# Scale and shift of the first normalisation: the conditioning product moved from GpSimd and VectorE to TensorE for five of eight tiles

## The chip, the cores and the metric

The kernel runs on one core of a Trainium2 chip. The metric is the device time of one execution in microseconds (us); three runs of the kernel before are given below, and one execution was profiled.

## The reference, cut to what matters

One decoder layer on x of shape (1, 1024, 1024) in float32. A conditioning vector c of 1024 numbers makes six vectors of 1024; the first two of them shift and scale the first normalisation, and what comes out goes into a wide projection:

```python
c_act = jax.nn.silu(c)
mod = c_act @ w_ada[l] + b_ada[l]                 # (1, 6*1024)
sh1, sc1, gt1, sh2, sc2, gt2 = jnp.split(mod, N_MOD, axis=-1)
h = _rmsnorm(x, norm1_g[l]) * (1.0 + sc1) + sh1
proj = h @ w_in[l]                                # RWKV, attention and gate columns
...                                               # two mixers, an output projection, an MLP
```

Only `sh1` and `sc1` are touched by the change: 2 x 1024 columns of `w_ada`, 8 MB, each summed over 1024 rows with `c_act` as weights.

## The kernel before, in words

The channels (1024) are cut into eight tiles of 128, numbered k = 0 to 7, and the same 1024 rows of `w_ada` into eight pieces j. For each k the kernel does, in this order:

- `ada_load(k)` loads the tile `wa`k: for each of the eight pieces j, 128 rows by 2 x 128 columns (scale, shift), in two transfers of 512 KB on SP's queue. `wa` has three buffers, so the fourth load waits for the first tile to be used up.
- `ada_sum(k)` makes the two sums. GpSimd multiplies three of the eight pieces by `cact` in one instruction (L277) and adds them into one (L279, two instructions); VectorE multiplies and adds the other five (L283, L285) into `acc`. TensorE then sums `acc` over its 128 partitions by two matmuls against a column of ones, one for scale and one for shift, each with one output column (`gp<-ones,acc`; L41 is the helper `mm` through which all matmuls but transposes go). VectorE turns `gp` into the two columns of `gs`k (L292, L293).
- `modulate(k)` transposes the normalised x of tile k on TensorE (eight 128x128 transposes into `xp`, L302), ScalarE evicts them with scale and shift from `gs`k into `hr` (L303), casts that to `hhi` (L304), and VectorE makes the remainder `hlo` (L305).
- `products(k)` adds tile k's share to three projections that are kept open in PSUM over all eight tiles: `p_wa`, `p_r` and `p_k`, each as hi x hi, lo x hi and hi x lo in two halves, 18 matmuls of 512 columns.

The loop calls `ada_sum(k+1)` and `modulate(k+1)` ahead of `products(k)`; a scheduler then sets the final order on each engine. Four PSUM banks of the tag `ps` serve `gp`, both halves of `xp` and `p_r`; two of them are held by `p_r` throughout, so `gp` and the halves of `xp` take turns in the other two. When the eight tiles are through, TensorE goes on with the projection `p_v`.

In the profile a float32 matmul appears as two MATMUL rows and two LDWEIGHTS rows (two matmuls `gp<-ones,acc` of a tile are four rows); a transpose, and a matmul on the split operands, is one.

Of the kernel before, what the change touches and what calls it, by code (L numbers as in the profile page):

```python
# [8 lines left out]
F32 = mybir.dt.float32  # L9
# [4 lines left out]
ALU = mybir.AluOpType  # L14
AX = mybir.AxisListType

P = 128
S = 1024
D = 1024
KT = 8  # L20
# [15 lines left out]
def build(ctx, tc, A, out):  # L36
    nc = tc.nc
    PE, ACT, DVE, POOL, SP = nc.tensor, nc.scalar, nc.vector, nc.gpsimd, nc.sync

    def mm(o, l, r, start, stop):  # L40
        PE.matmul(o, l, r, start=start, stop=stop)  # L41

    def pool(**kw):
        if kw.get("space") != bass.MemoryType.DRAM:
            kw["reuse_waits"] = "tile"
        return tc.tile_pool(**kw)
# [16 lines left out]
    def big(name, tag="pp"):  # L63
        return pools[tag][0].tile([P, pools[tag][1]], F32, tag=tag, name=name)

    def bank(name, tag="ps"):
        return big(name, tag)

    def halves_of(o):
        return [o[:, 0:512], o[:, 512:1024]]  # L70
# [7 lines left out]
    ones = const.tile([P, P], F32, name="ones")  # L78
# [47 lines left out]
    def vcol(name, i=0, n=1):  # L126
        vc, o = col[name]
        return vc[:, o + i : o + i + n]
# [9 lines left out]
    def small(name, n=1):  # L138
        return const.tile([P, n], F32, name=name)
# [5 lines left out]
    cact = small("cact", 8)  # L145
# [6 lines left out]
    def rsqrt(o, v, scale, eps, tmp, n):  # L152

        a, b = tmp[:, 0:n], tmp[:, n : 2 * n]
        ACT.activation(o, v, AF.Sqrt, bias=eps, scale=scale)
        DVE.tensor_scalar(a, v, scale, eps, ALU.mult, ALU.add)
        DVE.reciprocal(o, o)
        DVE.tensor_tensor(b, o, o, ALU.mult)
        DVE.tensor_tensor(b, b, a, ALU.mult)
        DVE.tensor_scalar(b, b, -0.5, 1.5, ALU.mult, ALU.add)  # L160
        DVE.tensor_tensor(o, o, b, ALU.mult)
# [21 lines left out]
    def win(c0, n=P):  # L183
        return w_in[:, :, c0 : c0 + n]
# [41 lines left out]
    with pool(name="st", bufs=1) as st:  # L226
        ssq = st.tile([P, 8], F32, name="ssq")
        rs1 = st.tile([P, 8], F32, name="rs1")
        rtmp = st.tile([P, 16], F32, name="rtmp")
        xs, was, gs, firsts = [], [], [], []  # L230

        def x_load(t):
            xt = st.tile([P, D], F32, name=f"x{t}")
            SP.dma_start(xt, x_t[t])
            xs.append(xt)

        def ada_load(k):
            wa = st.tile([P, KT, 2, P], F32, tag="wa", name=f"wa{k}", bufs=3)
            SP.dma_start(wa[:, :, 0, :], w_ada[:, :, D + k * P : D + (k + 1) * P])
            SP.dma_start(wa[:, :, 1, :], w_ada[:, :, k * P : (k + 1) * P])  # L240
            was.append(wa)

        def first_load(name, parts, to):
            raw = to.tile([P, KT, P], F32, tag="wraw", name=f"wr_{name}", bufs=2)
            for i, part in enumerate(parts):
                w_ = P // len(parts)
                SP.dma_start(raw[:, :, i * w_ : i * w_ + w_], part)
            return raw

        def first_tile(name, raw, to, banks):  # L250
            hi = to.tile([P, KT, P], F32R, tag="whi", name=f"wh_{name}", bufs=2)
            lo = to.tile([P, KT, P], F32R, tag="wlo", name=f"wl_{name}", bufs=2)
            ACT.copy(hi, raw)
            DVE.tensor_tensor(lo, raw, hi.bitcast(F32), ALU.subtract)
            o = [bank(f"p_{name}{hf}") for hf in range(2)] if banks else halves_of(big(f"p_{name}"))
            firsts.append(((hi, lo), o))

        def normalise(g):
            ts = slice(4 * g, 4 * g + 4)
            for t in range(4 * g, 4 * g + 4):  # L260
                junk = st.tile([P, D], F32, tag="junk", name=f"jk{t}", bufs=2)
                ACT.activation(junk, xs[t], AF.Square, accum_out=ssq[:, t : t + 1])
            rsqrt(rs1[:, ts], ssq[:, ts], 1.0 / D, eps1, rtmp, 4)
            for t in range(4 * g, 4 * g + 4):
                r = rs1[:, t : t + 1]
                if g:
                    ACT.activation(xs[t], xs[t], AF.Copy, scale=r)
                else:
                    DVE.tensor_scalar(xs[t], xs[t], r, None, ALU.mult)

        NPOOL = 3

        def ada_sum(k):

            wa, c0 = was[k], KT - NPOOL
            rest = wa[:, c0:].rearrange("p k i n -> p k (i n)")
            POOL.tensor_tensor(rest, rest, cact[:, c0:].unsqueeze(2).broadcast_to([P, NPOOL, 2 * P]), ALU.mult)  # L277
            for j in range(c0 + 1, KT):
                POOL.tensor_tensor(wa[:, c0], wa[:, c0], wa[:, j], ALU.add)  # L279
            acc = st.tile([P, 2, P], F32, tag="acc", name=f"acc{k}", bufs=3)  # L280
            for j in range(c0):
                if j == 0 and k == 0:
                    DVE.tensor_scalar(acc, wa[:, j], cact[:, j : j + 1], None, ALU.mult)  # L283
                else:
                    DVE.scalar_tensor_tensor(acc, wa[:, j], cact[:, j : j + 1], acc if j else wa[:, c0], ALU.mult, ALU.add)  # L285
            gp = bank(f"gp{k}")
            for i in range(2):
                mm(gp[:, i : i + 1], acc[:, i, :], ones[:, 0:1], True, k > 0)
                if k == 0:
                    mm(gp[:, i : i + 1], wa[:, c0, i, :], ones[:, 0:1], False, True)  # L290
            g_ = st.tile([P, 2], F32, name=f"gs{k}")
            DVE.tensor_scalar(g_[:, 0:1], gp[:, 0:1], bsc1[:, k : k + 1], vcol("g1", k), ALU.add, ALU.mult)  # L292
            DVE.tensor_scalar(g_[:, 1:2], gp[:, 1:2], vcol("bsh1", k), None, ALU.add)  # L293
            gs.append(g_)

        def modulate(k):
            hr = st.tile([P, S], F32, tag="hr", name=f"hr{k}", bufs=2)
            for hf in range(2):
                sl = slice(hf * 512, hf * 512 + 512)
                xp = bank(f"xp{k}_{hf}")  # L300
                for t in range(4):
                    PE.transpose(xp[:, t * P : (t + 1) * P], xs[4 * hf + t][:, k * P : (k + 1) * P], ident)  # L302
                ACT.activation(hr[:, sl], xp, AF.Identity, bias=gs[k][:, 1:2], scale=gs[k][:, 0:1])  # L303
            ACT.copy(hhi[:, k, :], hr)  # L304
            DVE.tensor_tensor(hlo[:, k, :], hr, hhi[:, k, :].bitcast(F32), ALU.subtract)  # L305

        def products(k):
            for w, o in firsts:
                for a, b in ((0, hhi), (1, hhi), (0, hlo)):
                    for hf in range(2):  # L310
                        sl = slice(hf * 512, hf * 512 + 512)
                        mm(o[hf], w[a][:, k, :], b[:, k, sl], k == 0 and a == 0 and b is hhi, k == KT - 1 and b is hlo)

        for t in range(8):
            x_load(t)
        ada_load(0)
        raws = [first_load("wa", [win(COL_WD, 64), win(COL_AD, 64)], st)]
        raws.append(first_load("r0", [win(COL_R)], st))
        raws.append(first_load("k0", [win(COL_K)], wp))
        ada_load(1)  # L320
        normalise(0)
        normalise(1)
        ada_sum(0)
        first_tile("wa", raws[0], st, False)
        modulate(0)
        first_tile("r0", raws[1], st, True)
        first_tile("k0", raws[2], wp, False)
        for k in range(KT):
            if k + 1 < KT:
                if k:  # L330
                    ada_load(k + 1)
                ada_sum(k + 1)
                modulate(k + 1)
            products(k)
            if k == 5:
                omu, hbase, kmh, kmo = second_columns()
# [759 lines left out]
    raw1, first, sums, rest = {}, {}, {}, {}  # L1096
# [368 lines left out]
    with pool(name="fr", bufs=1, side="right") as fr, pool(name="fp", bufs=1) as fp:  # L1465
        raws = {"B21": nx["b"]}
        acc = []
# [130 lines left out]
        for s, (g, i) in enumerate(flat):  # L1598
# [7 lines left out]
            tag, opens, _, _, to = STEPS[i]  # L1606
# [49 lines left out]
```

## Time and profile before

| | us |
|---|---|
| three runs: median (lowest to highest) | 1697.89 (1694.49 to 1701.91) |
| the profiled execution's own time | 1695.92 |
| its span in the trace | 1694.2 |
| TensorE busy, of the span | 1597.7 (94%) |
| VectorE, ScalarE, GpSimd busy | 1129.7, 731.2, 356.2 |

The span is what the trace covers from the first to the last instruction; 1.7 us of the time lie outside it. The busy time of TensorE counts matmuls whose ends are modelled, so durations of single matmuls overlap: the cost of one in a row of its kind is read from start to start. [...]

### The profile page before, as it was taken

To read this page: it belongs to the slowest core of one execution; us is meant where nothing else is said; L and a number is where in the kernel's file an instruction comes from. 1 tells how busy PE (TensorE), PEld (TensorE's weight loads), DVE (VectorE), ACT (ScalarE), POOL (GpSimd) and SP (SyncE) were. 2 spreads that over 40 slices of the span, in tenths; PEclk is the share of its full clock that TensorE was granted. 3 is DMA by queue.
4 is the path that set the end of the run, shared out by engine and by line. 5 is a ranking of instruction groups with operands and counts; after the bars stand their busy time and mean duration, and the time that the engine had idled before them with its cause. 6 is when DMAs were issued, how large, how long until landed. Compare 5 with 4: busy or idle time off the path is not lost.

```text
span 1694.2 us, 21870 instructions
## 1 busy us (share of the span) xinstructions
PE 1597.7 (94%) x8293; PEld 1277.9 (75%) x8293; DVE 1129.7 (67%) x1685; ACT 731.2 (43%) x1138; POOL 356.2 (21%) x353
## 2 busy tenths in 40 slices
PE   3999998999999999999999999999999969999997
PEld 2767766777777878888887787777777857888886
DVE  6677665556665735666647655975555569899978
ACT  5454432444454723333233334755555524433334
POOL 4410000699992011121110000122211100000000
PEclk9999999999999999999999999999999989999999
DMA  8535333622223168778767421344444474364522
GB/s 248 139 100 152 114 121 124 154 55 68 62 79 108 42 193 250 225 234 240 231 210 242 168 100 63 126 157 150 147 156 160 149 274 160 124 224 154 170 75 100
DMA packets 217111, 256.24 MB, mean 151 GB/s; under 512 B 30097, under 2 KB 156330, under 8 KB 216878
## 3 DMA queue, kind: packets, MB, share of 16 engines
q1 hardware_dynamic: 205390, 214.71, 41.6%
q0 software_dynamic: 11408, 39.85, 6.2%
q8 instruction: 65, 1.06, 0.3%
q14 instruction: 40, 0.33, 0.1%
q10 hardware_dynamic: 208, 0.28, 0.0%
HBM read 178.16 MB, written 72.45 MB: 148 GB/s over the span
## 4 chain that ended last, share of the span: by engine, by line
PE 62%; issue 14%; DVE 7%; DMA 6%; POOL 3%; ACT 2%; SPq 0%; POOLq 0%; DVEq 0%; ACTq 0%
PE x L1215 11%; PE y L1215 8%; PE p_gb L41 5%; PE p_out L41 5%; PE p_ga L41 3%; POOL f_d L1230 3%; PE my L41 3%; PE p_fk L41 3%; PE p_ob L41 3%; PE p_fq L41 2%; PE p_fv L41 2%; PE yv L41 2%; PE p_v L41 2%; PE p_r L41 2%; PE tp L819 2%
## 5 line engine op out<-in xcount | busy, mean ns | idle before, releaser
L1404 ACT CAST dh<-dA 128x1024 fp32r<-128x1024 f32 x54 | 56.3, 1046 | 148.0 <-PE x L1215 72.2
L1215 PE MATMUL x<-wh,dh 128*128 128x512 f32 x256 | 102.1, 399 | 14.5 <-ACT wh L1093 14.5
L639 POOL TENSOR_TENSOR dg<-dg,inv 128x62 f32<-128x62 f32 (+30 forms) x62 | 100.2, 1617 | 4.8
L1215 PE MATMUL x<-wl,dh 128*128 128x512 f32 x256 | 100.9, 395 | 0.0
L1215 PE MATMUL x<-wh,fl 128*128 128x512 f32 x256 | 100.1, 391 | 0.0
L638 POOL TENSOR_TENSOR inv<-dg 128x62 f32<-128x62 f32 (+30 forms) x62 | 92.9, 1498 | 4.9
L1583 DVE TENSOR_TENSOR fl<-dA,dh 128x1024 fp32r<-128x1024 f32 x54 | 65.2, 1218 | 20.7 <-ACT dh L1404 14.7
L1215 PE MATMUL y<-wh,dh 128*128 128x512 f32 x176 | 69.4, 394 | 0.0
L1215 PE MATMUL y<-wl,dh 128*128 128x512 f32 x176 | 68.6, 393 | 0.6 <-DVE wl L1094 0.6
L1215 PE MATMUL y<-wh,fl 128*128 128x512 f32 x176 | 68.3, 388 | 0.0
L1215 PEld LDWEIGHTS x<-wh,dh 128*128 128x128 f32 x256 | 48.8, 191 | 24.6 <-ACT wh L1093 14.9
L823 DVE TENSOR_TENSOR pl<-tp,ph 128x512 fp32r<-128x512 f32 (+1 forms) x80 | 49.1, 631 | 24.8 <-ACT ph L822 24.6
L879 DVE CUSTOM_DVE_ANT_0 pt<-s,cb 128x512 f32<-128x512 f32 (+2 forms) x64 | 36.4, 584 | 37.4 <-PE s L41 36.5
L881 ACT ACTIVATE pt<-pt,sm 128x128 f32<-128x128 f32 (+3 forms) x64 | 49.5, 775 | 24.5 <-DVE sm L879 23.5
L701 POOL TENSOR_TENSOR sw<-sbd,wcs 64x256 f32<-64x256 f32 x28 | 22.8, 816 | 169.1 <-DVE sbd L702 138.4
L1239 ACT ACTIVATE ff<-ff 128x512 f32<-128x512 f32 x48 | 30.3, 632 | 64.7 <-DVE ff L1325 29.3
L1215 PEld LDWEIGHTS x<-wl,dh 128*128 128x128 f32 x256 | 48.3, 189 | 12.0 <-DVE wl L1094 0.5
L1215 PEld LDWEIGHTS x<-wh,fl 128*128 128x128 f32 x256 | 48.7, 190 | 10.7
L822 ACT CAST ph<-tp 128x512 fp32r<-128x512 f32 (+1 forms) x80 | 41.5, 543 | 29.2 <-PE tp L819 27.6
L41 PE MATMUL p_out<-h_wo,hhi 128*128 128x512 f32 x128 | 50.8, 397 | 2.2 <-ACT h_wo L1050 2.2
L41 PE MATMUL p_gb<-hhi,wl_gb 128*128 128x512 f32 x128 | 51.4, 402 | 0.2 <-DVE wl_gb L178 0.2
L819 PE MATMUL tp<-ident,pt 128*128 128x128 f32 x288 | 49.6, 282 | 2.2 <-ACT pt L881 1.8
(584 smaller groups left out, 4909.5 us busy)
## 6 DMA issues: line engine op xcount, KB each, us to landing
dA<-f_d SPq DMA_DIRECT2D x27, 1024.0 KB
aw<-in_w_ada SPq DMA_DIRECT2D x32, 512.0 KB
ur<-in_w_ff SPq DMA_DIRECT2D x30, 512.0 KB
B<-in_w_ff SPq DMA_DIRECT2D x15, 1024.0 KB
f_d<-ff POOLq DMA_DIRECT2D x48, 256.0 KB, 4.1
wa<-in_w_ada SPq DMA_DIRECT2D x16, 512.0 KB
sc_d<-scb SPq DMA_DIRECT2D x16, 512.0 KB
sct<-sc_d SPq DMA_DIRECT2D x16, 512.0 KB
```

What stands on the lines that cost most here:

```text
L41: PE.matmul(o, l, r, start=start, stop=stop)
L638: POOL.tensor_tensor(tv, dg[:, 0:s, s : s + 1].broadcast_to([P, s, m]), dg[:, s : s + 1, s + 1 :].broadcast_to([P, s, m]), ALU.mult)
L639: POOL.tensor_tensor(dg[:, 0:s, s + 1 :], dg[:, 0:s, s + 1 :], tv, ALU.add)
L819: PE.transpose(tp[:, x * P : (x + 1) * P], pr[b][:, t * P : (t + 1) * P], ident)
L822: ACT.copy(ph[:, 0:w_], tp[:, 0:w_])
L823: DVE.tensor_tensor(pl[:, 0:w_], tp[:, 0:w_], ph[:, 0:w_].bitcast(F32), ALU.subtract)
L879: DVE.tensor_tensor_reduce(pt[:, c0:c1], sv, cb[:, c0:c1], -0.125, low, ALU.add, ALU.min, st_[:, x : x + 1])
L881: ACT.activation(pt[:, 0:n], pt[:, 0:n], AF.Exp, bias=low, scale=-1.0, accum_out=ls[:, b : b + 1])
L1215: PE.matmul(o, l, r, start=start, stop=stop, skip_group_check=True)
L1230: POOL.dma_start(f_d[AOPS.index(name), j], src)
L1404: ACT.copy(hs[i], src[:, 2 * i : 2 * i + 2])
L1583: DVE.tensor_tensor(fl[:, sl], src[:, sl], f32(hs[i_]), ALU.subtract)
```

## The change

TensorE multiplies `w_ada`'s pieces by the conditioning itself for tiles 0, 1, 3, 5 and 7: 16 matmuls with one output column each (eight pieces, scale and shift), the piece as the loaded operand and a column of `cact` as the moving one. For tiles 2, 4 and 6 VectorE does all eight pieces (eight instructions where there were five) and TensorE the two matmuls against ones as before. GpSimd does none. `wa` gets a fourth buffer and `acc` loses one; tiles 1 to 3 are loaded ahead of the loop, and the load of tile k+4 comes after the sum of tile k+1.

```diff
         def ada_load(k):
-            wa = st.tile([P, KT, 2, P], F32, tag="wa", name=f"wa{k}", bufs=3)
+            wa = st.tile([P, KT, 2, P], F32, tag="wa", name=f"wa{k}", bufs=4)
...
-        NPOOL = 3
-
         def ada_sum(k):
-            wa, c0 = was[k], KT - NPOOL
-            rest = wa[:, c0:].rearrange("p k i n -> p k (i n)")
-            POOL.tensor_tensor(rest, rest, cact[:, c0:].unsqueeze(2).broadcast_to([P, NPOOL, 2 * P]), ALU.mult)
-            for j in range(c0 + 1, KT):
-                POOL.tensor_tensor(wa[:, c0], wa[:, c0], wa[:, j], ALU.add)
-            acc = st.tile([P, 2, P], F32, tag="acc", name=f"acc{k}", bufs=3)
-            for j in range(c0):
-                if j == 0 and k == 0:
-                    DVE.tensor_scalar(acc, wa[:, j], cact[:, j : j + 1], None, ALU.mult)
-                else:
-                    DVE.scalar_tensor_tensor(acc, wa[:, j], cact[:, j : j + 1], acc if j else wa[:, c0], ALU.mult, ALU.add)
+            wa = was[k]
             gp = bank(f"gp{k}")
-            for i in range(2):
-                mm(gp[:, i : i + 1], acc[:, i, :], ones[:, 0:1], True, k > 0)
-                if k == 0:
-                    mm(gp[:, i : i + 1], wa[:, c0, i, :], ones[:, 0:1], False, True)
+            if k < 2 or k % 2:
+                for i in range(2):
+                    for j in range(KT):
+                        mm(gp[:, i : i + 1], wa[:, j, i, :], cact[:, j : j + 1], j == 0, j == KT - 1)
+            else:
+                acc = st.tile([P, 2, P], F32, tag="acc", name=f"acc{k}", bufs=2)
+                for j in range(KT):
+                    if j == 0:
+                        DVE.tensor_scalar(acc, wa[:, j], cact[:, j : j + 1], None, ALU.mult)
+                    else:
+                        DVE.scalar_tensor_tensor(acc, wa[:, j], cact[:, j : j + 1], acc, ALU.mult, ALU.add)
+                for i in range(2):
+                    mm(gp[:, i : i + 1], acc[:, i, :], ones[:, 0:1], True, True)
...
-        ada_load(1)
+        for k in (1, 2, 3):
+            ada_load(k)
...
         for k in range(KT):
             if k + 1 < KT:
-                if k:
-                    ada_load(k + 1)
                 ada_sum(k + 1)
+                if k + 4 < KT:
+                    ada_load(k + 4)
                 modulate(k + 1)
```

The order moves on TensorE. The first place is the start of the stage, from the sums of tile 0 to those of tile 1. Before, TensorE ran twelve matmuls of tile 0's products while VectorE and GpSimd made tile 1's sums:

```order
L302 MATMUL xp0_1_228<-ident_72,x7_146 128x128
L41 MATMUL p_wa_220<-hhi_124,wh_wa_216 128x512 x2
L41 MATMUL p_wa_220<-hhi_124,wl_wa_217 128x512 x2
L41 MATMUL p_k0_246<-hhi_124,wh_k0_242 128x512 x2
L41 MATMUL p_wa_220<-hlo_125,wh_wa_216 128x512 x2
L41 MATMUL p_k0_246<-hhi_124,wl_k0_243 128x512 x2
L41 MATMUL p_k0_246<-hlo_125,wh_k0_242 128x512 x2
L41 MATMUL gp1_256<-ones_77,acc1_250 128x1 x2
L302 MATMUL xp1_0_263<-ident_72,x0_132 128x128
```

In the changed kernel there stands at the same place:

```order
L299 MATMUL xp0_1_237<-ident_72,x7_146 128x128
L41 MATMUL p_wa_229<-hhi_124,wh_wa_225 128x512
L41 MATMUL gp1_256<-cact_118,wa1_158 128x1 x8
L299 MATMUL xp1_0_280<-ident_72,x0_132 128x128
L299 MATMUL xp1_0_280<-ident_72,x1_134 128x128
L299 MATMUL xp1_0_280<-ident_72,x2_136 128x128
L299 MATMUL xp1_0_280<-ident_72,x3_138 128x128
L299 MATMUL xp1_1_286<-ident_72,x4_140 128x128
L41 MATMUL gp1_256<-cact_118,wa1_158 128x1 x8
```

Of tile 0's 18 products one now stands ahead of tile 1's sums and transposes and 17 behind them, in one piece; the other twelve no longer fill the time in which tile 1's sums were made.

The second place is tile 3, the first of the later tiles whose sums go to TensorE. Before:

```order
L41 MATMUL p_k0_246<-hlo_125,wh_k0_242 128x512 x2
L41 MATMUL gp3_358<-ones_77,acc3_352 128x1 x2
L302 MATMUL xp3_0_365<-ident_72,x0_132 128x128
L302 MATMUL xp3_0_365<-ident_72,x1_134 128x128
L302 MATMUL xp3_0_365<-ident_72,x2_136 128x128
L302 MATMUL xp3_0_365<-ident_72,x3_138 128x128
L41 MATMUL p_wa_220<-hhi_124,wh_wa_216 128x512 x2
L302 MATMUL xp3_1_371<-ident_72,x4_140 128x128
```

In the changed kernel:

```order
L41 MATMUL p_k0_255<-hlo_125,wh_k0_251 128x512 x2
L41 MATMUL gp3_363<-cact_118,wa3_164 128x1 x16
L299 MATMUL xp3_0_387<-ident_72,x0_132 128x128
L299 MATMUL xp3_0_387<-ident_72,x1_134 128x128
L299 MATMUL xp3_0_387<-ident_72,x2_136 128x128
L299 MATMUL xp3_0_387<-ident_72,x3_138 128x128
L299 MATMUL xp3_1_393<-ident_72,x4_140 128x128
L299 MATMUL xp3_1_393<-ident_72,x5_142 128x128
...
L41 MATMUL p_wa_229<-hhi_124,wh_wa_225 128x512 x2
```

Sixteen one-column matmuls stand where two stood, and all eight transposes of the tile follow them in one piece. Behind tile 7 the order of TensorE's instructions is that of before.

## Rows read from the trace of the kernel before

**Rows 1.** Windows: busy us of PE, PEld, DVE, ACT, POOL; clock, DMA share, GB/s.

```profile
10.00:20.00 10.00, 0.00 (x0) 0.00 (x0) 6.85 (x19) 8.84 (x16) 1.90 (x2) 1.00 1.16 309
...
35.00:40.00 5.00, 1.26 (x6) 0.77 (x5) 4.06 (x4) 0.00 (x0) 4.52 (x5) 1.00 0.00 0
...
55.00:60.00 5.00, 5.00 (x30) 4.24 (x29) 4.60 (x9) 2.28 (x4) 2.10 (x2) 1.00 0.04 11
```

**Rows 2.** Timeline: start, us, engine, instruction, count, [idle before, releaser]; tiles 0 and 1.

```profile
17.95 0.35 DVE L283 TENSOR_SCALAR acc<-wa,cact 128x256 f32<-128x256 f32 x1 [0.60 <-DMA wa<-in_w_ada]
...
23.95 1.95 PE L302 MATMUL xp<-ident,x 128*128 128x128 f32 x8
...
27.48 1.47 POOL L277 TENSOR_TENSOR wa<-wa,cact 128x768 f32<-128x768 f32 x1 [6.11 <-DMA wa<-in_w_ada]
...
28.64 1.22 PE L41 MATMUL p_wa<-hhi,wh_wa 128*128 128x512 f32 x2 [2.75 <-ACT hhi L304]
...
39.23 1.01 PE L41 MATMUL gp<-ones,acc 128*128 128x1 f32 x4 [3.74 <-DVE acc L285]
...
40.11 1.95 PE L302 MATMUL xp<-ident,x 128*128 128x128 f32 x8
...
41.11 2.05 DVE L285 SCALAR_TENSOR_TENSOR acc<-wa,cact,acc 128x256 f32<-128x256 f32 x4
```

**Rows 3.** Timeline of TensorE alone, from tile 0's last products on.

```profile
41.70 1.20 PE L41 MATMUL p_r<-hhi,wh_r 128*128 128x512 f32 x2
...
43.56 1.05 PE L41 MATMUL p_r<-hlo,wh_r 128*128 128x512 f32 x2
44.41 0.62 PE L41 MATMUL p_wa<-hhi,wh_wa 128*128 128x512 f32 x1
44.84 0.53 PE L41 MATMUL gp<-ones,acc 128*128 128x1 f32 x4
45.23 0.64 PE L302 MATMUL xp<-ident,x 128*128 128x128 f32 x4
...
53.25 0.66 PE L302 MATMUL xp<-ident,x 128*128 128x128 f32 x4 [1.70 <-DVE gs L293]
```

**Rows 4.** The same: one whole tile, a wait, the stage's end.

```profile
57.48 0.50 PE L41 MATMUL gp<-ones,acc 128*128 128x1 f32 x4
57.84 0.63 PE L302 MATMUL xp<-ident,x 128*128 128x128 f32 x4
...
62.47 0.63 PE L41 MATMUL p_k<-hlo,wh_k 128*128 128x512 f32 x2
62.94 0.50 PE L41 MATMUL gp<-ones,acc 128*128 128x1 f32 x4
...
65.16 0.66 PE L302 MATMUL xp<-ident,x 128*128 128x128 f32 x4 [0.99 <-DVE gs L293]
...
85.50 0.47 PE L41 MATMUL p_v<-hhi,wh_v 128*128 128x512 f32 x1 [0.16 <-DVE wa_t L446]
```

**Rows 5.** Timeline of TensorE: eight one-column matmuls in a row, much later.

```profile
808.67 1.84 PE L41 MATMUL ac<-ones,aa 128*128 128x1 f32 x16
810.37 1.14 PE L41 MATMUL my<-sbd,art 128*128 128x128 f32 x8
```

**Rows 6.** Windows of 1 us after an idle TensorE; columns as in the first windows.

```profile
165.00:166.00 1.00, 0.00 (x0) 0.00 (x0) 1.00 (x1) 0.00 (x0) 0.00 (x0) 1.00 0.45 163
...
167.00:168.00 1.00, 1.00 (x10) 1.00 (x10) 1.00 (x2) 0.49 (x2) 0.00 (x0) 0.88 0.06 17
168.00:169.00 1.00, 1.00 (x7) 1.00 (x6) 0.03 (x1) 0.58 (x2) 0.00 (x0) 0.50 0.00 0
...
171.00:172.00 1.00, 1.00 (x3) 0.42 (x3) 0.00 (x0) 0.62 (x2) 0.00 (x0) 0.91 0.99 320
```

**Rows 7.** Timeline of TensorE: another idle stretch, then sixteen transposes alone.

```profile
270.23 3.58 PE L593 MATMUL bp<-ident,bk 128*128 128x128 f32 x16 [3.97 <-DVE bk L589]
273.55 0.49 PE L41 MATMUL p_f<-hlo,wfs 128*16 128x512 f32 x1
```

**Rows 8.** Windows of 1 us over those transposes; columns as in the first windows.

```profile
271.00:272.00 1.00, 1.00 (x7) 1.00 (x6) 0.43 (x1) 0.59 (x1) 0.00 (x0) 0.50 0.00 0
...
274.00:275.00 1.00, 1.00 (x6) 0.38 (x4) 0.00 (x0) 0.00 (x0) 0.00 (x0) 1.00 0.99 338
```

## The prediction

> **What bounds the kernel now.** I read the page first: TensorE is busy for 94% of the span, so elsewhere its own work sets the time, and what it is given more to do comes back in the end unless it fills a gap. The change lies in the first 86 us, so I went there by windows. In [rows 1] the reader sees three different pictures: from 10 to 20 us TensorE does nothing while 309 GB/s come in; from 35 to 40 us it works 1.26 us of 5 and the DMA share is 0.00, so it isn't the loads that are waited for there; from 55 to 60 us it is busy without a gap. The timeline tells what ends the waits. Tile 0's coefficients come from `wa0`, whose last half VectorE gets at 17.95; the tile's transposes start at 23.95, its first product at 28.64, released by ScalarE's cast. Tile 1's sums start at 39.23, after 3.74 us of waiting for `acc` [rows 2]. From 41.70 on TensorE runs on, but for two waits for VectorE's `gs`, 1.70 us at 53.25 and 0.99 us at 65.16, until `p_v` begins at 85.50 [rows 3, 4]. So two things count: when tile 1 gets going, and TensorE's work per tile after that.
>
> The clock is part of it. [...]
>
> **The start (tiles 0 and 1).** Tile 0: the sums by VectorE and GpSimd, 17.95 to 22 us, make way for 32 rows on TensorE (16 float32 matmuls, two rows each). At the low level a one-column row costs 0.22 us (four from 39.23 to 40.11 [rows 2]), so 7.0 us, plus eight transposes at 0.20 (40.11 to 41.70 [rows 2, 3]), 1.6: 8.6 us. If both halves of `wa0` are there only at 17.95, this ends at 26.6, against 23.95 + 1.6 = 25.6 now; but the sums of scale need only the first half, 512 KB earlier, 1.7 us at the 309 GB/s of [rows 1], and then it ends at 24.9. I take nothing, bounds -0.7 and +1.0 us.
>
> Tile 1: TensorE starts again at 28.64 and now has one product (0.43), 32 one-column rows (7.0) and eight transposes (1.6) before the other 17 products of tile 0: 37.7. Its tile `wa1` is there by 27.48 [rows 2], and the queue ahead of it is the same. The 17 products: with the low level for 3.1 us more, as from 41.70 to 44.84, 7.4 of them at 0.425, then 9.6 at 0.235, together 5.4: done at 43.1. Now tile 0's last product ends at 44.41. **Term 1: -1.3 us.** Bounds: all 17 at the low level, 7.2, so 44.9 (+0.5); or the clock rising while the one-column rows run, which is a rival below (-4.5).
>
> **The later tiles.** The work per tile is read from 57.48 to 62.94 [rows 4]: 5.46 us, of it 0.36 the four `gp` rows. Tiles 3, 5 and 7 get 32 rows instead. What does one cost at the full level, in a row of many? The nearest row is of exactly this kind, eight one-column matmuls with new loaded operands: 16 rows from 808.67 to 810.37, 0.106 us each [rows 5]. So 32 x 0.106 = 3.4, less 0.36, is 3.04 per tile. **Term 2: +9.1 us.** Bounds: 0.09 a row as in the short groups (0.36 / 4) gives +7.6; 0.22, were the clock low throughout, +20. Tiles 2, 4 and 6 keep their two matmuls.
>
> [...]
>
> **VectorE, GpSimd and the loads.** VectorE's eight multiply-adds of an even tile cost about 0.51 each undisturbed (four in 2.05 us at 41.11 [rows 2]), 4.1 us, and lie under at least one tile's TensorE work of 5.46; without that cover an even tile would wait up to 4.1 us for them. VectorE had five for each of eight tiles and now has 24 in all, and GpSimd none, so `gs` should no longer be late: the waits of 1.70 and 0.99 go. New ones come: the second half of `xp` uses the bank that `gp` leaves, and in tile 3 only four transposes stand between, so TensorE waits for two small VectorE instructions; tile 2's `hlo` also comes closer to its use. I put 1.0 us for all, bounds 0 and 2.7. **Term 3: -1.7 us.** The loads get earlier, into a time when the DMA share was 0.00; `vr_b` and `p_v`'s weights now queue on SP behind the last `w_ada` tile, which waits for tile 3's sums to leave its buffer, and are used only at the stage's end: nothing. GpSimd's work leaves no path.
>
> **Sum.** -1.3 + 9.1 - 1.7 = +6.1 us at the end of the stage. `p_v` follows it with 0.16 us of waiting, and the order behind is unchanged, so it stays: 1695.9 + 6.1 = 1702.0 against the profiled execution's own time. That time is 2.0 below the median of the three runs, from which the sum is 1704.0. I say 1703.
>
> **Rivals.** *The clock falls.* Tiles 3, 5 and 7 now have 3.4 us of one-column rows and then up to eight transposes. After an idle stretch the granted clock fell to 0.50 for 3.4 us (0.88 in the slice from 167, 0.91 in that from 171: 0.24 + 3 + 0.18 [rows 6]); if one-column rows count as little as idling, it falls in each of the three tiles. 3.4 us at half speed cost 1.7: +5.1 in all, 1695.9 + 6.1 + 5.1 = 1707; were all the one-column rows at 0.22, 11 more on the sum, 1713. For it: nothing in the trace has so long a stretch of one column. Against it: 1.7 us of them at 808.67 cost 0.106 a row throughout, and during sixteen transposes alone (270.23 to 273.55) the clock came back from 0.50 to 1.00 [rows 7, 8], so short matmuls that each load an operand do count for something. It decides (slower by over 0.5%, past 1704.4 on the same basis) from the second tile in which it happens. [...] Chance 0.25.
>
> *The clock rises early.* TensorE has no pause from 28.64 on. Before, the full level came 5.6 us after 39.23. If one-column rows count fully, it comes at 34.2: three of the second sixteen rows are through, 13 at 0.106 and the last transposes end at 35.9, 17 products at 0.235 at 39.9, 4.5 ahead of now: -4.5 + 9.1 - 1.7 = +2.9, 1699. Against it: from 39.23 to 41.70 the one-column rows and transposes did not raise it. Chance 0.2.
>
> *The loss is taken up behind the stage.* Then 1696. VectorE idles there at times, but TensorE's waits behind the stage are for chains that start from it; chance 0.08.
>
> Could it be faster by over 0.5%? With the early rise, 0.09 a row and no new wait: -4.5 + 7.6 - 2.7 = +0.4. The best bounds together give no gain, as the three tiles put back what the start saves.
>
> **How the numbers follow.** The sum as it stands has 0.42; 0.05 is left for what I do not see. 0.5% (8.5 us) is about what a measurement here can tell from no change, given that the three runs differ by 7.4. The range goes from the early rise with some spread, 1696, to a fall in most tiles, 1711. Slower by over 0.5%: 0.2 of the falling clock and 0.05 of the sum's upper end, 0.25; faster 0.03; the same 0.72.
>
> **What would show it.** Term 1: tile 0's last product near 43 us, one-column rows of tile 1 at 0.22. Term 2: sixteen matmuls (32 rows) of tiles 3, 5 and 7 in 3.4 us each, clock 1.00. Term 3: no wait for `gs` over 0.5 us. `p_v` should start near 91.6. Wrong would be: a clock of 0.50 between 45 and 90 us, one-column rows far from 0.106, or tile 1's products at 0.235 from the first.

## The result, and the profile after

The changed kernel takes 1711.37 us in the median of eight runs (1706.74 to 1715.47) against 1698.86 for the kernel before, measured beside it (eight runs, 1694.49 to 1705.18): ratio 1.0062, 95% interval 1.0043 to 1.008, so 12.5 us slower by the medians. That is 8 us past the number forecast and at the very end of its range (1696 to 1711, passed by 0.4), on the side of the rival called the falling clock. The forecast gave 0.72 to a change within 0.5% and 0.25 to a kernel slower by more than that; the second is what came.

The profiled execution after took 1715.47, the longest of its eight, and the one before 1695.92, 2.9 under its kernel's median. The two traces are therefore 19.6 us apart where the medians are 12.5 apart. 13.84 of this is there at `p_v`. Behind it the shift is still 14.0 where the transposes `hp` begin (987.3, now 1001.3). Another 5.2 come between `hp` and the first matmul of `x`, a stretch of 398.0 us before and 403.2 after, which took 397.0 to 404.3 over all the profiles here with no order by kernel; it isn't explained here.

The timeline of TensorE after, from tile 0's first product to `p_v`:

```profile
start us, us, engine line op out<-in xcount [idle before <-releaser]
28.09 0.80 PE L41 MATMUL p_wa<-hhi,wh_wa 128*128 128x512 f32 x1 [2.96 <-ACT hhi L301]
28.69 3.41 PE L41 MATMUL gp<-cact,wa 128*128 128x1 f32 x16
31.95 1.31 PE L299 MATMUL xp<-ident,x 128*128 128x128 f32 x5
33.05 3.41 PE L41 MATMUL gp<-cact,wa 128*128 128x1 f32 x16
...
42.33 0.62 PE L41 MATMUL p_k<-hlo,wh_k 128*128 128x512 f32 x2
42.79 0.63 PE L41 MATMUL p_wa<-hhi,wh_wa 128*128 128x512 f32 x2
...
47.80 0.62 PE L41 MATMUL p_k<-hlo,wh_k 128*128 128x512 f32 x2
48.26 4.06 PE L41 MATMUL gp<-cact,wa 128*128 128x1 f32 x32
52.18 1.95 PE L299 MATMUL xp<-ident,x 128*128 128x128 f32 x8
53.78 1.20 PE L41 MATMUL p_wa<-hhi,wh_wa 128*128 128x512 f32 x2
...
65.46 4.18 PE L41 MATMUL gp<-cact,wa 128*128 128x1 f32 x32
...
82.94 4.75 PE L41 MATMUL gp<-cact,wa 128*128 128x1 f32 x32
...
99.34 0.47 PE L41 MATMUL p_v<-hhi,wh_v 128*128 128x512 f32 x1
```

The start is as forecast: the one-column rows of tile 1 cost 0.20 us each (sixteen from 28.69 to 31.95), and tile 0's last product is through at 42.79, where before it was through at 44.41 [rows 3]. After 28.09 no row up to `p_v` has a wait in brackets, the rows left out here included, so the waits for `gs` of 1.70 and 0.99 us [rows 3, 4] are gone. Yet `p_v` starts at 99.34 instead of 85.50. The windows over the same execution show why (the number before the DMA share is the granted clock):

```profile
core 0: us, PE busy (x) PEld busy (x) DVE busy (x) ACT busy (x) POOL busy (x), PEclk, DMA share, GB/s
50.00:51.00 1.00, 1.00 (x11) 1.00 (x11) 0.00 (x0) 0.00 (x0) 0.00 (x0) 1.00 0.00 0
51.00:52.00 1.00, 1.00 (x8) 1.00 (x9) 0.00 (x0) 0.00 (x0) 0.00 (x0) 0.64 0.00 0
52.00:53.00 1.00, 1.00 (x6) 1.00 (x7) 0.64 (x3) 0.00 (x0) 0.00 (x0) 0.50 0.00 0
...
57.00:58.00 1.00, 1.00 (x4) 0.81 (x3) 1.00 (x3) 0.00 (x0) 0.00 (x0) 0.50 0.24 55
58.00:59.00 1.00, 1.00 (x5) 0.82 (x5) 0.04 (x1) 0.00 (x0) 0.00 (x0) 0.95 0.01 2
...
68.00:69.00 1.00, 1.00 (x8) 1.00 (x7) 0.00 (x0) 0.00 (x0) 0.00 (x0) 0.67 0.00 0
...
75.00:76.00 1.00, 1.00 (x5) 0.77 (x4) 0.03 (x1) 0.00 (x0) 0.00 (x0) 0.91 0.00 0
...
85.00:86.00 1.00, 1.00 (x8) 1.00 (x9) 0.00 (x0) 0.00 (x0) 0.00 (x0) 0.71 0.10 20
...
92.00:93.00 1.00, 1.00 (x5) 0.86 (x4) 0.61 (x1) 0.36 (x1) 0.62 (x1) 0.88 0.57 154
```

TensorE is busy for 1.00 of every slice, and still the clock falls to 0.50 three times, once in each of tiles 3, 5 and 7, while the one-column rows run. The slice from 51 has 0.72 us at the low level, those from 52 to 58 six, the slice from 58 0.10: 6.8 us. The other two lows are as long, 20.5 us in all. A pair of products takes 0.86 us at 0.50 (55.63 to 56.49, where every slice reads 0.50) and 0.46 at 1.00 (42.33 to 42.79 above), so about half of a low is lost, by estimate 10.2 us. With the working of the prediction this closes to about a microsecond: -1.6 at the start, +9.1 for the rows, +10.2 for the clock, -2.9 for the waits that are gone (1.70, 0.99 and the 0.16 before `p_v`) make +14.8, measured +13.84.

### The profile page after: what moved, and what is told of

The parts are those of the page before. It is cut to its first block, busy times and chain, and to the rows that moved or that the text cites. A ratio compares the mean times of both kernels' runs of the same rounds, so it can differ in the third digit from the quotient of the medians.

```text
span 1713.8 us, 22086 instructions
## 1 busy us (share of the span) xinstructions
PE 1627.9 (95%) x8429; PEld 1307.5 (76%) x8429; DVE 1111.7 (65%) x1669; ACT 731.5 (43%) x1138; POOL 327.6 (19%) x329
## 4 chain that ended last, share of the span: by engine, by line
PE 65%; issue 14%; DVE 8%; DMA 6%; POOL 3%; ACT 3%; SPq 0%; POOLq 0%; ACTq 0%; DVEq 0%
PE x L1213 11%; PE y L1213 7%; PE p_gb L41 5%; PE p_out L41 5%; PE p_ga L41 3%; POOL f_d L1228 3%; PE my L41 3%; PE p_r L41 3%; PE p_ob L41 3%; PE p_fq L41 2%; PE p_k L41 2%; PE p_fv L41 2%; PE p_fk L41 2%; PE yv L41 2%; PE p_v L41 2%
## 5 line engine op out<-in xcount | busy, mean ns | idle before, releaser
L1213 PE MATMUL y<-wh,fl 128*128 128x512 f32 x176 | 68.3, 388 | 0.0
L41 PE MATMUL p_ga<-hhi,wh_ga 128*128 128x512 f32 x128 | 51.4, 401 | 0.0
```

The lines of the kernel that those rows point to most:

```text
L1213: PE.matmul(o, l, r, start=start, stop=stop, skip_group_check=True)
```

## The experiments

The theory: one-column rows that stand alone for about 3.5 us let the clock fall, and their own price is as forecast. The rivals: the transposes behind them do it, or the float32 operand loads, or the loss is not the clock's but one of VectorE's or of the start. Ratios are to the kernel before, measured beside each. A start of `p_v` is from one execution.

**128 equal columns in place of one, all five tiles.** The moving operand is the same column of `cact` repeated; the matmuls and operand loads are as many, the sums the same.

```diff
+        cb = st.tile([P, KT, P], F32, name="cb")
+        DVE.tensor_copy(cb, cact.unsqueeze(2).broadcast_to([P, KT, P]))
...
-                        mm(gp[:, i : i + 1], wa[:, j, i, :], cact[:, j : j + 1], j == 0, j == KT - 1)
+                        mm(gp[:, i * P : i * P + P], wa[:, j, i, :], cb[:, j, :], j == 0, j == KT - 1)
```

> As the changed kernel, but each of TensorE's sixteen matmuls per tile (tiles 0, 1, 3, 5, 7) moves 128 equal columns (cact repeated) instead of one; same number of rows, same loaded operands. Theory (TensorE's one-column rows do not keep the clock at its full level: 20.5 us at the low level between 51 and 92 us cost some 10 of the 13.8 us that the stage lost): granted clock 1.00 from 45 to 90 us, a row still about 0.11 us, p_v starts at 88 to 91 us instead of 99.3, and the time is 8 to 12 us below the changed kernel's 1711, about 1700. Rival (it is the work of the rows and the longer wait for the coefficients, the clock is a side show): p_v at 99 or later, time 1711 or more.

Measured: 1697.21 us (five runs), ratio 0.9951 [0.9928, 0.9975], `p_v` at 83.42. TensorE's timeline, and windows over tiles 3, 5 and 7:

```profile
41.46 3.74 PE L41 MATMUL gp<-cb,wa 128*128 128x128 f32 x32
45.03 0.60 PE L303 MATMUL xp<-ident,x 128*128 128x128 f32 x4
...
55.73 3.73 PE L41 MATMUL gp<-cb,wa 128*128 128x128 f32 x32
```

```profile
41.00:46.00 5.00, 5.00 (x42) 4.71 (x41) 3.59 (x8) 0.27 (x1) 0.00 (x0) 1.00 0.76 186
55.00:60.00 5.00, 5.00 (x42) 4.79 (x41) 1.72 (x4) 1.05 (x2) 0.00 (x0) 1.00 0.43 115
69.00:75.00 6.00, 6.00 (x48) 5.29 (x47) 1.19 (x8) 0.52 (x1) 0.62 (x1) 1.00 0.00 0
```

32 rows take 3.57 us (41.46 to 45.03), nearly what they take with one column at the full level (3.49, in a profile further down), and the clock stays at 1.00. The operand loads and the transposes are the same, so neither of them let it fall by itself here. The gain went further than expected since the start gained too: tile 0's last product is through at 35.8 instead of 42.8.

**One-column rows in the first two tiles only, and in the later three only.** In the first run tiles 2 to 7, in the second tiles 0 and 1, are again split between VectorE (five pieces) and GpSimd (three); tiles 2, 4 and 6 of the second stay whole on VectorE, as in the changed kernel. The condition of each run (the rest of the edits is left out):

```diff
-            if k < 2 or k % 2:
+            if k < 2:                 # first two
+            if k > 1 and k % 2:       # later three
```

> TensorE makes the sums of tiles 0 and 1 alone; tiles 2 to 7 are shared by VectorE and GpSimd as before. Theory: only the gain of the start is left (tile 0's products end about 1.6 us sooner, no waits for gs), clock 1.00 after 42 us, p_v at 81 to 84 us against 85.5 before, time 1694 to 1699, not to be told from before or a little faster. Rival (the loss comes with the new loading order and the sums of tiles 0 and 1): p_v later than 90 us, time over 1705.

> TensorE makes the sums of tiles 3, 5 and 7 alone; tiles 0 and 1 are shared by VectorE and GpSimd as before; 2, 4 and 6 on VectorE as in the changed kernel. Theory: the whole loss and none of the gain: three stretches at clock 0.50, p_v at 99 to 104 us, time 1710 to 1717. Rival (the sums of tiles 0 and 1 carry the loss): p_v below 90, time about 1700.

Measured: first two 1695.41 us (five runs), 0.9943 [0.9923, 0.9963], `p_v` at 84.55, just past what was expected; the granted clock reads 1.00 up to `p_v` and the waits for VectorE are back (the longest 1.48 for `gs`). Later three 1702.03 us (ten runs), 1.0011 [0.9981, 1.0042], `p_v` at 96.4, three lows, of 3.4, 6.8 and 6.8 us. Both its numbers are below what was expected, the time by 8 us. In part this is because tile 1's sums came to TensorE at 36.1 rather than 39.23 [rows 2] and one low was half as long; the rest isn't explained. At `p_v` the loss is in the later tiles; the time of the second can't be told from the kernel before.

**The operands exchanged**: the column of `cact` is loaded and 256 columns of `w_ada` move, all five tiles; two small matmuls bring the row back to columns.

```diff
+                for j in range(KT):
+                    mm(gp[0:1, 0 : 2 * P], cact[:, j : j + 1], wa[:, j].rearrange("p i n -> p (i n)"), j == 0, j == KT - 1)
+                DVE.tensor_copy(rw, gp[0:1, 0 : 2 * P])
```

> As the changed kernel, but operands swapped: a column of cact is loaded and a piece's 256 columns of w_ada move (16 rows per tile instead of 32), and two small matmuls turn the resulting row back into two columns. Theory (what keeps the clock up is columns that move): a row about 0.12 us, sums of a tile 1.9 us at the full level, clock 1.00 from 40 us on, p_v at 77 to 81 us, time 1690 to 1696. Rival (a matmul that fills one column of the array counts as little as one that moves one column): the clock stays low at the start until the 512-column products come, p_v at 83 to 88 us, time about 1698.

Measured: 1699.74 us (ten runs), 0.9991 [0.9968, 1.0013], `p_v` at 88.49, no low in tiles 3, 5 and 7. `p_v` and the time missed the theory's numbers because the price of a row did. Tile 3's row of the timeline,

```profile
44.57 3.61 PE L41 MATMUL gp<-wa,cact 128*1 128x256 f32 x16
48.12 0.66 PE L303 MATMUL xp<-ident,x 128*128 128x128 f32 x4
```

has 16 rows from 44.57 to 48.12, 0.222 us for 256 columns, where 0.12 was expected. A row of 512 columns on the split operands takes 0.23 (two in 0.46 from 42.33 to 42.79 above). The float32 row of 256 columns thus cost about twice as much per column, and the two rows of a matmul four times.

**The one-column matmuls of tiles 5 and 7 put between the 512-column products**, tile 3's left in one piece.

```diff
                         mm(o[hf], w[a][:, k, :], b[:, k, sl], k == 0 and a == 0 and b is hhi, k == KT - 1 and b is hlo)
+                        if extra is not None:
+                            next(extra, None)
```

> As the changed kernel, but the sixteen one-column matmuls of tiles 5 and 7 are each put between 512-column products of an earlier tile; those of tile 3 still stand in one piece. Same work. Theory: the clock falls once, in tile 3 (some 6.8 us at 0.50), and not in tiles 5 and 7; p_v at 91 to 94 us, time about 1704. Rival (work alone): p_v at 98 to 100, time 1711.

Measured: `p_v` at 93.28, as expected; one low, from 50.5 to 57.3, in tile 3's rows and behind them, none in tiles 5 and 7. This is one profile, with two such stretches. Windows over these two:

```profile
62.00:69.00 7.00, 7.00 (x50) 6.45 (x49) 3.76 (x8) 2.17 (x3) 0.00 (x0) 1.00 0.50 138
76.00:90.00 14.00, 14.00 (x82) 11.92 (x82) 4.62 (x11) 5.00 (x6) 2.90 (x6) 1.00 0.32 79
```

The time, 1710.7 us (seven runs; 1.0042 [1.0007, 1.0077]), was a miss by 7: `p_v` came 6 us earlier than in the profile after (0.8 earlier than in the second one, below), and the median gained nothing that can be told. The stretch from `hp` to `x` was 403.0 us in its profile; what else came back isn't known.

**The start alone, two more ways**: 128 columns, and exchanged operands, for tiles 0 and 1; the rest split as before.

> TensorE makes the sums of tiles 0 and 1 alone, with 128 moving columns per row; tiles 2 to 7 are shared by VectorE and GpSimd as before. Theory: the early clock of the run with 128 columns (tile 0's products done at 35.8 us) without the 3 x 3.2 us of rows in tiles 3, 5 and 7, so p_v at 74 to 78 us and a time of 1688 to 1693, below both kernels. Rival (VectorE and GpSimd then set the pace, their sums take as long as a tile): waits for gs of 1 to 3 us per tile, p_v at 80 to 84, time 1695 to 1699.

> TensorE makes the sums of tiles 0 and 1 alone, with swapped operands (a column of cact loaded, 256 columns moving); tiles 2 to 7 are shared by VectorE and GpSimd as before. Theory: half as many rows at the start, so tile 1's sums end sooner than with 128 equal columns; p_v at 73 to 77 us, time 1687 to 1692. Rival (VectorE and GpSimd set the pace, or the clock does not rise early): p_v at 80 to 84, time 1695 to 1699.

Measured: 1694.21 (0.9964 [0.9944, 0.9985], `p_v` 82.1) and 1694.82 (0.9965 [0.9938, 0.9992], `p_v` 84.4), twelve runs each. Both missed on `p_v`, and the rival came: TensorE, now early, waited for VectorE. Behind such waits the clock fell as well, in the first from 37.9 to 44.7 (TensorE had waited 2.09 us to 37.69), though not after the longest wait there, 2.91 us to 56.60; in the second at 42.0 and at 52.2 for 3.4 us each. TensorE's waits in the first (us in total, times, longest):

```profile
PE xp L305 <- DVE gs L296: 2.9, 1, 2.9
PE p_wa L41 <- DVE hlo L308: 2.1, 1, 2.1
...
PE gp L41 <- DVE acc L290: 2.0, 1, 2.0
```

**Half of the columns each**: 128 columns in tiles 0 and 1 alone, then in tiles 3, 5 and 7 alone; the sums are divided among engines as in the changed kernel.

```diff
-                        mm(gp[:, i : i + 1], wa[:, j, i, :], cact[:, j : j + 1], j == 0, j == KT - 1)
+                        n = P if k < 2 else 1              # start;  P if k > 1 and k % 2 else 1  for later
+                        mm(gp[:, i * n : i * n + n], wa[:, j, i, :], cb[:, j, 0:n], j == 0, j == KT - 1)
```

> The changed kernel with 128 equal moving columns in the scale and shift matmuls of tiles 0 and 1 alone; tiles 3, 5 and 7 keep one column. It splits the gain of the kernel with 128 columns throughout (p_v at 83.4 us against 99.3) between the start and the later tiles. Theory (the one-column rows let the clock fall wherever they stand alone for 3 us or more, and at the start they also keep it from rising): at the start the full level comes near 29 us and tile 0's last product near 35 instead of 42.3; three stretches at 0.50 of about 7 us each remain in tiles 3, 5 and 7, 3.4 us of loss each, so p_v at 91 to 94 and a time of 1702 to 1707. Rival (what the earlier start gains is given back, because VectorE's sums of tiles 2, 4 and 6 are then late): p_v at 97 or later, with waits of TensorE for acc or gs of 2 us or more. If an earlier full clock keeps the gate from falling later, p_v comes near 84.

> The other half: one column in tiles 0 and 1 as in the changed kernel, 128 equal columns in tiles 3, 5 and 7. Theory: the start is as in the changed kernel, with tile 0's last product near 42.3 us; no stretch at 0.50 after it; the sixteen matmuls of tiles 3, 5 and 7 take 3.6 us each as with 128 columns throughout; p_v at 88 to 91 and a time of 1698 to 1703. Rival (the fall comes from the eight transposes that follow the rows, or from the wait for gs, not from the one-column rows): the stretches at 0.50 stay and p_v is later than 95. This kernel and the one with 128 columns in tiles 0 and 1 alone should together give the 15.9 us that 128 columns throughout gained at p_v.

Measured: start 1701.77 us (ten runs), 1.0019 [0.9997, 1.0042]; later 1701.52 (ten runs), 1.0018 [0.9998, 1.0038]. Of the changed kernel's 1.0062 the first takes back 0.43% and the second 0.44%, and both together (the kernel with 128 columns throughout) 1.1%. The second came as expected. TensorE's timeline in it:

```profile
47.72 3.73 PE L41 MATMUL gp<-cb,wa 128*128 128x128 f32 x32
...
62.10 3.73 PE L41 MATMUL gp<-cb,wa 128*128 128x128 f32 x32
...
76.59 3.84 PE L41 MATMUL gp<-cb,wa 128*128 128x128 f32 x32
...
89.89 0.47 PE L41 MATMUL p_v<-hhi,wh_v 128*128 128x512 f32 x1
```

No stretch is at 0.50 up to `p_v`, and `p_v` is 4.4 us behind the kernel before. The first was a miss: `p_v` at 85.53, not 91 to 94, because only tile 7's rows were followed by a low. That is nearer to the last possibility named for it, that an earlier full clock keeps the clock from falling later. Tiles 3 and 5, with the same rows as in the changed kernel, ran at 1.00. Tile 3's rows in the timeline, then windows:

```profile
42.36 3.63 PE L41 MATMUL gp<-cb,wa 128*128 128x1 f32 x32
45.85 0.63 PE L304 MATMUL xp<-ident,x 128*128 128x128 f32 x4
```

```profile
42.00:46.00 4.00, 4.00 (x37) 3.91 (x36) 1.12 (x1) 0.00 (x0) 0.00 (x0) 1.00 0.66 161
56.00:60.00 4.00, 4.00 (x36) 3.90 (x35) 0.02 (x1) 0.00 (x0) 0.00 (x0) 1.00 0.77 213
74.00:75.00 1.00, 1.00 (x10) 0.93 (x10) 0.47 (x5) 0.00 (x0) 0.00 (x0) 1.00 0.00 0
75.00:76.00 1.00, 1.00 (x6) 0.84 (x5) 0.22 (x3) 0.57 (x1) 0.71 (x1) 0.50 0.06 23
```

So the theory was too simple: the rows don't let the clock fall every time. The next two runs ask what decides it.

**The changed kernel and the one with the wide start, unaltered, profiled a second time.**

> The changed kernel as it is, for a second profile. In its first profile the clock fell in each of tiles 3, 5 and 7; in the kernel with 128 columns in tiles 0 and 1 the very same one-column rows let it fall in tile 7 alone. Theory (whether the clock falls is settled by the place in time at which the rows happen to stand, which the program does not fix): another execution shows other falls, two or three stretches at 0.50 in tiles 3, 5 and 7, beginning at other moments relative to the rows, p_v at 95 to 100. Rival (the program settles it): the same three stretches to within 0.3 us of 51.3, 68.3 and 85.4, p_v within 0.3 us of 99.34.

> The kernel with 128 columns in tiles 0 and 1 and one column in tiles 3, 5 and 7, for a second profile. In its first profile tiles 3 and 5 ran at 1.00 throughout and only tile 7's rows were followed by a stretch at 0.50, p_v at 85.53. Theory (place in time, not fixed by the program): another set of tiles falls, and each fall adds 1.7 to 3.4 us at p_v: 83.5 with none, up to 94 with three. Rival (with the full clock reached at 31 us, tiles 3 and 5 never let it fall): the same picture, one fall near 74.7 us, p_v at 85.2 to 85.9.

Measured: the changed kernel 1711.55 us, `p_v` at 94.07 (99.34 in its first profile, 95 to 100 expected); the wide start 1703.85, `p_v` at 87.82 (85.53). Windows of the changed kernel's second profile:

```profile
49.00:50.00 1.00, 1.00 (x10) 1.00 (x10) 0.00 (x0) 0.06 (x1) 0.00 (x0) 0.92 0.30 73
...
56.00:57.00 1.00, 1.00 (x5) 0.79 (x4) 0.98 (x2) 0.27 (x1) 0.00 (x0) 0.67 1.22 298
64.00:69.00 5.00, 5.00 (x42) 4.78 (x40) 1.79 (x4) 0.00 (x0) 0.00 (x0) 1.00 0.30 77
...
83.00:84.00 1.00, 1.00 (x8) 0.85 (x8) 0.69 (x6) 0.00 (x0) 0.00 (x0) 0.98 0.00 0
84.00:85.00 1.00, 1.00 (x6) 1.00 (x5) 0.00 (x0) 0.87 (x2) 0.83 (x1) 0.50 0.00 0
...
87.00:88.00 1.00, 1.00 (x5) 0.77 (x5) 1.00 (x2) 0.00 (x0) 0.06 (x1) 0.81 0.86 177
```

Tile 3's rows (from 47.70) let the clock fall at 49.8 for 6.8 us, tile 5's (from 64.97) not at all, and tile 7's (from 79.31) at 84.0, when they were through, for 3.4 us. The sum made for the first profile closes here too: -2.2 at the start (42.24 against 44.41), +9.1 for the rows, +5.1 for half of 10.2 us of lows and -2.9 for the waits make +9.1, measured +8.57. In the wide start's second profile tile 3 stayed at 1.00, tile 5 fell at 60.2 for 3.4 us and tile 7 at 73.9 for 6.8. The slices in which they fell:

```profile
60.00:61.00 1.00, 1.00 (x6) 0.84 (x5) 0.00 (x0) 1.00 (x2) 0.00 (x0) 0.60 0.03 8
...
73.00:74.00 1.00, 1.00 (x11) 1.00 (x10) 0.00 (x0) 0.00 (x0) 0.00 (x0) 0.93 0.00 0
```

The same program gives other falls in another execution: so the rival, that the program settles it, is wrong, and an early full clock doesn't keep tile 5 from falling. What remains of the theory is that a stretch of one-column rows puts the clock at risk.

**Three wide tiles at the start**, the rest split as before: an attempt at a version that beats both kernels.

```diff
-            if k < 2 or k % 2:
+            if k < 3:                 # 128 columns here, five pieces VectorE and three GpSimd in the others
```

> 128 equal columns on TensorE for tiles 0, 1 and 2; tiles 3 to 7 split as in the kernel before, five multiply-adds on VectorE and three on GpSimd. With tiles 0 and 1 alone on TensorE, tile 2's sums came late (TensorE waited 2.0 us for acc and 2.9 for gs, and the clock fell for 6 us after). Theory (VectorE was late there because it had the first tiles' casts and tile 2's sums at once): tile 2's 3.6 us on TensorE replace those waits and the fall, clock 1.00 from 30 us on, p_v at 78 to 81 against 82.1 and 85.5 in the kernel before, a time of 1689 to 1694. Rival (VectorE and GpSimd remain late, now in tile 3): a wait for acc or gs of 2 us or more in tile 3, a stretch at 0.50 behind it, p_v at 82 to 85 and 1694 to 1698.

Measured: 1689.44 us (eight runs, 1685.67 to 1695.19), 0.9936 [0.9912, 0.996], faster than both kernels. The rival was right on the mechanism:

```profile
44.75 1.09 PE L305 MATMUL xp<-ident,x 128*128 128x128 f32 x4 [3.82 <-DVE gs L296]
...
84.21 0.47 PE L41 MATMUL p_v<-hhi,wh_v 128*128 128x512 f32 x1 [0.16 <-DVE wa_t L450]
```

The wait only went on to tile 3, with a low of 3.4 us behind it, and `p_v` is 1.3 us ahead of the kernel before [rows 4]. That doesn't account for 0.64% in the time; its interval overlaps those of the other early starts (0.9943 to 0.9965), and which of them is best stays open.

## Why the prediction was right or wrong

**What bounds the kernel** held: it is TensorE's work per tile after tile 1, with no wait left to hide anything.

**Term 1 (start, -1.3)**: right in size. Tile 0's last product was through at 42.8 in one profile and at 42.2 in the other, 43.1 forecast, all at 0.20 a row. Of the prices forecast for the 17 products, 0.425 is half of the pair from 43.56 to 44.41 [rows 3] and 0.235 half of that from 62.47 to 62.94 [rows 4]. The granted clock reads 1.00 at both, but a pair took 0.86 where it read 0.50 and 0.46 where it read 1.00 in the profile after; so the low level of the start, and its end near 44.84, is inferred from the spacing. The rival of the early rise didn't happen with one column; with 128 columns throughout it did (35.8), and gave 6 to 7 us.

**Term 2 (later tiles, +9.1) is the step that failed.** Its row price was right: at the full level 32 rows take 3.49 us (42.36 to 45.85 in the wide start) and 3.57 with 128 columns, 3.4 forecast. Wrong was to take the full level for granted. The row it rests on, eight matmuls in 1.70 us at 0.106 [rows 5], covers half the length, and a stretch of 1.7 us can't show what one of 3.4 does to the clock. In the two profiles of the changed kernel five of the six stretches fell, for 30.7 us together, and the term was nearer +19 in the first and +14 in the second. A clock of 0.50 between 45 and 90 us was the prediction's own sign of being wrong.

**Term 3 (waits, -1.7)**: the waits went as said; the new waits of 1.0 did not come, and the 0.16 before `p_v` went too, so it measured -2.9.

**The rival of the falling clock** was what happened, though it had only 0.25, and it did decide: without falls in tiles 3, 5 and 7 (the kernel with 128 columns there) the ratio is 1.0018. That the time still stands at the end of the range, and not far outside, is because the range took in this rival; the sum did not. Its size, 1.7 us lost in each of three tiles, 5.1, can be set against all stretches of one-column rows in tiles 3, 5 and 7 (fall: us after the first row):

| kernel, profile | tiles that fell | fall came after | low lasted |
|---|---|---|---|
| changed, first | 3, 5, 7 | 3.0, 2.9, 2.5 | 6.8, 6.8, 6.8 |
| changed, second | 3, 7 of 3, 5, 7 | 2.1, 4.7 | 6.8, 3.4 |
| later three only | 3, 5, 7 | 4.9, 2.9, 2.5 | 3.4, 6.8, 6.8 |
| spread in 5, 7 | 3 of 3 | 2.8 | 6.8 |
| wide start, first | 7 of 3, 5, 7 | 4.2 | 3.4 |
| wide start, second | 5, 7 of 3, 5, 7 | 4.6, 2.4 | 3.4, 6.8 |

12 of 16 stretches fell and were 68 us at half speed, so 34 us lost, 2.1 for each stretch, 6.4 for three. In the changed kernel's own two profiles it was 10.2 and 5.1, on average 7.7, so the 5.1 was small by a third and its agreement with the second profile is chance. With the wide start three of six fell, in the other kernels nine of ten; whether the start matters for this stays open with so few. Against these sixteen, none of six such stretches with 128 columns fell (the kernels with 128 columns throughout and in the later three), nor any of three with exchanged operands. The time agrees: 128 columns in tiles 3, 5 and 7 alone take the ratio from 1.0062 to 1.0018, 0.44% or 7.5 us (each of the two ratios is to other runs of the kernel before). What is left, 0.18% or 3 us, is the sum without the clock: +6.1 forecast, +4.4 at `p_v`.

**The argument against that rival** was that short matmuls which each load an operand count for something, from sixteen transposes that brought the clock back [rows 7, 8]. They move 128 columns each: they say something of the 128-column rows, which kept the clock (none of six fell), and nothing of one column. What transposes by themselves do to the clock isn't shown by the experiments: the same eight follow the rows in the kernels that fell and in those that didn't. There are only the sixteen of the kernel before: the slice from 273 us has 0.71, so the level rose at about 273.6, just as they ended (the next matmul is at 273.55 [rows 7]).

**The price of a float32 row** was the same with 1 column and with 128: 32 rows took 3.49 and 3.57 us, 0.11 each. With 256 columns, and another operand loaded, a row took 0.222. What sets the 0.11 isn't shown: no run here varies the operand load alone. The price of one column, and with it the sum, is not touched by this.

**Taken up behind the stage** didn't happen: 13.84 at `p_v` was still 14.0 at `hp` in the first profile, and 8.57 was 11.2 there in the second.

## What to carry to other kernels

The work moved to TensorE had two prices here: its own rows, and what it did to the clock of the dense matmuls behind it, which was the larger of the two in the first profile (10.2 against 9.1 us) and the smaller in the second (5.1). The price per row read from a burst of 1.70 us said nothing on the clock in one twice as long, where 12 of 16 stretches fell; if matmuls of one column have to stand alone for microseconds, give them columns that cost next to nothing (128 here took 3.57 us where one took 3.49, and none of six stretches fell). Putting them between dense ones kept the clock in the two stretches tried, but no gain in time could be told. Take two profiles before a clock is called a property of a program.

## What the runs showed of the hardware

A busy share of 1.00 didn't keep the clock: in the changed kernel's first profile it fell to 0.50 at 51.3, 68.3 and 85.4 us with TensorE at 1.00 in every slice. The stretches that fell here (12 of 16) had one moving column; otherwise equal ones with 128 did not fall (none of six).

Whether and when a stretch let it fall wasn't fixed by the program: the changed kernel's second profile has falls at 49.8 and 84.0 us and none in tile 5, and of the two with the wide start the first has one at 75.0, the second at 60.2 and 73.9. What decides it isn't shown. In these and the other profiles of the table the eight falls that came 2.1 to 3.0 us after the first row stayed 6.8 us, and the four that came after 4.2 to 4.9 us, when the rows were through, stayed 3.4.

Over its eight runs the changed kernel's time goes with the mean granted clock of the execution, 1706.74 us at 0.987 to 1715.47 at 0.982, but for one (1714.84 at 0.984). The kernel before has a wider spread without such rows (25 runs, 1691.86 to 1707.8 us at 0.983 to 0.991), so differences of a few us between two single profiles, at `p_v` too, are to be read with care.
